# First feed-forward of a hybrid transformer block: its input products by seven half-size products, its output in pieces of two, two modulation vectors computed later

## Chip, cores, metric

One core of one Trainium2 chip runs the whole kernel. The metric is the device time of one execution in microseconds (us), the median of three runs. Engines are named as in the profile: PE (matrix multiplications; PEld is its loading of weights), DVE (vector), ACT (scalar), POOL, SP (which issues the DMAs).

## What is computed

One transformer block on 512 tokens `x` and 256 context tokens `ctx` of width 1024, all in float32. A vector `c` gives nine modulation vectors; each of the three stages normalises and modulates its input and adds its gated, normalised output:

```python
mod = (silu(c) @ w_ada + b_ada).reshape(B, 9, 1, 1024)          # mod_c likewise from c_ctx
swiglu = lambda h, w_in, w_out: (silu(h @ w_in[:, :2816]) * (h @ w_in[:, 2816:])) @ w_out
h  = rmsnorm(x, g0) * (1 + m[1]) + m[0];   x = x + 0.5 * m[2] * rmsnorm(swiglu(h, ffn1), p0)     # ctx too
h  = rmsnorm(x, g1) * (1 + m[4]) + m[3];   y = mixer(h, hc)     # window attention + gated scan, two merged
x  = x + m[5] * rmsnorm(y, p1)
h  = rmsnorm(x, g2) * (1 + m[7]) + m[6];   x = x + 0.5 * m[8] * rmsnorm(swiglu(h, ffn2), p2)
mixer's end:  y = (sigmoid(ga) * (o_att @ w_o_attn) + sigmoid(gr) * (o_rec @ w_o_hgrn)) @ w_out
```

## The kernel before

Every float32 operand of a product is split into a high part (a cast on ACT) and a low part (a subtraction on DVE), `split`, L64 to L66; a product is three matmuls, high by high, high by low, low by high (`mm3`, L71, L72, L74).

**FFN1** works on all 768 tokens. The 2816 columns between the layers are 22 tiles j of 128. For each j, `in_tile` in `ffn` makes the gate and the up projection: 8 steps over the width, each with 512 and 256 tokens of 3 matmuls, so 96 matmuls a tile. Its output `am` is split into `acth` and `actl`. The output product (`out_phase`) takes tiles in pieces, PIECES = (1, 3, 3, 3, 3, 3, 2, 4): for each of the six groups of 128 tokens and each tile of the piece 6 matmuls of 512 columns, summed in PSUM, and then added to `tok` on DVE (L369). A piece's output product is written behind the first input tile of the next piece. The last piece goes to `last1`, which finishes each token group and transposes it for the mixer (`post`, `pre_xn`, `make_hT`; this stretch is called the tail below).

**FFN2** works on 512 tokens, and makes its input products in another way, `ffn7`. After two ordinary tiles it computes each tile j by seven products of half the width by half the tokens (a Strassen-Winograd scheme): sums of quarters of the input (`sums2`, once) and of the weights (`weights`, L408 to L411, for each j), 7 x 4 x 3 = 84 matmuls of 256 tokens (`product`, L421 to L423), and additions of the results on DVE as they leave PSUM (L478 to L493). The quarters of the input, plain and summed, each split in two, are called forms.

**Modulation** is not done by PE. A generator goes through `w_ada` in tiles `wa` of 128 x 512 (two buffers) and multiplies and adds them into `macc` on DVE (L611, L613) for one or two vectors; a matmul with ones then sums over partitions, and the result is combined with `b_ada` (L658) or turned into columns (L636, L639). `tick(n)` runs such generators from the list `background` for n units of credit, one unit an accumulation. The first modulation is computed in the start. In FFN1's background stand gate 0 (x and ctx), columns 1 (x and ctx), gate 1 and columns 2; FFN2's background has gate 2.

**The mixer** ends in a merge loop: for each of 8 column tiles the two gates' projections and the two output projections, multiplied and added on DVE (L1100 to L1102) and split (`mgl`); then the y product with `w_out`.

Only the beginning is ordered by hand; from the first matmuls on a scheduler lays out each engine's instructions ahead of time, and each engine runs its own list in order. SP issues all DMAs of one list in order too, so a load that waits for its buffer holds up those behind it.

Of the kernel before, what the change touches and what calls it, by code (L numbers as in the profile page):

```python
# [43 lines left out]
def kernel(ctx: ExitStack, tc: tile.TileContext, i, out):  # L44
# [109 lines left out]
    xT = ct([P, KD, TA], "xT", pool=st)  # L154
# [80 lines left out]
    def make_hT(n, hh, hl, toks, xns, pool, tag="h32"):  # L235
# [9 lines left out]
        for k in range(KD):  # L245
# [57 lines left out]
    def ffn(w_in, w_out, hT, groups, ntok, pool, pieces, yacc, last, groups0=None, pre=None, ticks=0, final_pre=None,  # L303
            order=None):

        gmax = max(b - a for a, b in groups)
        early = []

        def in_w(j, u):
            return split_w(load_w(w_in[:, u * FF + j * P:u * FF + (j + 1) * P]))  # L310

        def in_tile(j):
            if j == 0:
                early.extend(proj_all(pre, hT, groups0 or groups, by_k=not groups0))
            gs_ = groups
            if early:
                g = early.pop(0)
            else:
                w = in_w(j, 0)
                tick(ticks)  # L320
                g = proj(w, hT, groups)
            if early:
                u = early.pop(0)
            else:
                w = in_w(j, 1)
                tick(ticks)
                u = proj(w, hT, groups)
            ah = ct([P, ntok * P], "acth", F32R, bufs=4, pool=pool)
            al = ct([P, ntok * P], "actl", F32R, bufs=4, pool=pool)
            for gp, up, (a, b) in zip(g, u, gs_):  # L330
                s = ct([P, gmax], "sg", bufs=2, pool=pool)
                nc.scalar.activation(s[:, :b - a], gp, AF.Silu)  # L332
                m = ct([P, gmax], "am", bufs=2, pool=pool)
                nc.vector.tensor_tensor(out=m[:, :b - a], in0=s[:, :b - a], in1=up, op=ALU.mult)  # L334
                split(ah[:, a:b], al[:, a:b], m[:, :b - a])
            return ah, al

        run_pieces(in_tile, w_out, ntok, pool, pieces, yacc, last, final_pre, order)

    def run_pieces(in_tile, w_out, ntok, pool, pieces, yacc, last, final_pre=None, order=None, w4=None):  # L340
# [52 lines left out]
    F_B11, F_B21, F_B22, F_U1, F_U2, F_T3, F_T4 = range(7)  # L393
    H4 = KD // 2

    def ffn7(w_in, w_out, forms, nt, ntok, pool, w4, pieces, yacc, last, pre, sums, nstd=2, ticks=0):
# [37 lines left out]
        def act(up):  # L434
            ah = ct([P, ntok * P], "acth", F32R, bufs=4, pool=pool)
            al = ct([P, ntok * P], "actl", F32R, bufs=4, pool=pool)
            split(ah, al, up.rearrange("p a b -> p (a b)"))
            return ah, al

        def std_tile(j):  # L440
            if j == 0:
                early.extend(ps() for _ in pre)
                for half in range(2):
                    for o, w in zip(early, pre):
                        std_half(o, w, half)
# [820 lines left out]
```

## Time and profile before

| | us |
|---|---|
| median of 3 runs (lowest to highest) | 1485.39 (1485.19 to 1489.04) |
| the profiled execution: own time | 1484.94 |
| the profiled execution: span in the trace | 1483.2 |
| mean granted PE clock, of full speed | 0.992 |
| FFN1, from the second input tile to the last input product | 67.80 to 579.98 |
| tail of FFN1 | 580 to 640 |
| merge loop and y product | 960 to 1166 |
| FFN2 | 1167 to the end |

The span lies 1.74 us inside the profiled execution's own time. An engine's busy time counts its instructions in execution; overlapping ones are counted once.

### The profile page before, as it was taken

What the parts mean: (1) busy time and instruction counts of PE and PEld (TensorE: products, weight loads), DVE (VectorE), ACT (ScalarE), POOL (GpSimd) and SP (SyncE); (2) the same over time, 40 slices, a digit from 0 to 9 for tenths busy, and PEclk for the clock granted to TensorE, in tenths of its full rate; (3) what the DMA queues carried; (4) which work ended last, traced back from release to release, by engine and by line L of the source; (5) the groups of instructions that cost most, each with busy time, mean ns of one, the idle gap of its engine ahead of it and who ended that gap; (6) DMA issues with size and microseconds to landing.
All of it is one profiled execution on the core that took longest, in us unless ns stands there. A gap on an engine that the chain in (4) does not pass through costs nothing.

```text
span 1483.2 us, 22466 instructions
## 1 busy us (share of the span) xinstructions
PE 1428.8 (96%) x9064; PEld 1227.1 (83%) x9064; DVE 982.1 (66%) x1601; ACT 583.2 (39%) x973; POOL 59.0 (4%) x87
## 2 busy tenths in 40 slices
PE   5999999999999999999999989999999999999997
PEld 2688888888888888788889867788778889999996
DVE  6856664675655333848578579853448987787785
ACT  6532121212121222543234468842237544454442
POOL 3200000000000000200000200000001000000001
PEclk9999999999999999999999989999999999999999
DMA  9564331454552211222122211023242643243211
GB/s 309 173 201 130 114 114 58 128 164 142 168 164 63 67 29 57 68 86 64 39 58 59 63 54 46 24 77 99 83 131 91 214 136 100 86 138 103 88 43 57
DMA packets 177904, 151.57 MB, mean 102 GB/s; under 512 B 6408, under 2 KB 152328, under 8 KB 177800
## 3 DMA queue, kind: packets, MB, share of 16 engines
q1 hardware_dynamic: 177800, 150.14, 33.3%
q8 instruction: 71, 1.16, 0.3%
q14 instruction: 33, 0.27, 0.1%
HBM read 148.02 MB, written 2.10 MB: 101 GB/s over the span
## 4 chain that ended last, share of the span: by engine, by line
PE 70%; issue 16%; DVE 7%; ACT 3%; DMA 2%; POOL 2%; DVEq 0%; POOLq 0%; ACTq 0%; SPq 0%
PE mm L71 18%; PE mm L74 18%; PE mm L72 18%; PE mm L421 2%; PE mm L423 2%; PE mm L422 2%; PE aux L421 2%; PE aux L422 2%; PE aux L423 2%; PE aux L1046 1%; POOL rs L227 1%; DVE wl L66 1%; DMA mx<-b_ada 1%; DMA wa<-w_ada 1%; POOL ss L226 1%
## 5 line engine op out<-in xcount | busy, mean ns | idle before, releaser
L71 PE MATMUL mm<-hh,wh 128*128 128x512 f32 (+1 forms) x1128 | 389.9, 347 | 0.5 <-ACT sg L332 0.2
L72 PE MATMUL mm<-hl,wh 128*128 128x512 f32 (+1 forms) x1128 | 368.9, 344 | 0.0
L74 PE MATMUL mm<-hh,wl 128*128 128x512 f32 (+1 forms) x1128 | 325.5, 346 | 0.7 <-DVE wl L66 0.7
L66 DVE TENSOR_TENSOR wl<-wraw,wh 128x1024 fp32r<-128x1024 f32 (+1 forms) x159 | 189.3, 1196 | 171.7 <-ACT wh L65 170.3
L65 ACT CAST wh<-wraw 128x1024 fp32r<-128x1024 f32 (+1 forms) x159 | 162.7, 1029 | 352.0 <-PE mm L72 238.0
L71 PEld LDWEIGHTS mm<-hh,wh 128*128 128x128 f32 x1128 | 212.6, 189 | 46.1 <-ACT gg L911 0.7
L72 PEld LDWEIGHTS mm<-hl,wh 128*128 128x128 f32 x1128 | 213.1, 189 | 27.4 <-DVE hl L541 0.6
L74 PEld LDWEIGHTS mm<-hh,wl 128*128 128x128 f32 x1128 | 185.8, 190 | 9.3 <-DVE wl L66 1.1
L71 PE MATMUL mm<-woh,acth 128*128 128x512 f32 x420 | 164.2, 391 | 0.9 <-DVE am L334 0.9
L72 PE MATMUL mm<-wol,acth 128*128 128x512 f32 x420 | 164.0, 391 | 0.0
L613 DVE SCALAR_TENSOR_TENSOR macc<-wa,cs,macc 128x512 f32<-128x512 f32 x140 | 101.7, 749 | 51.0 <-DMA wa<-w_ada 50.3
L74 PE MATMUL mm<-woh,actl 128*128 128x512 f32 x420 | 130.8, 390 | 0.0
L65 ACT CAST woh<-w 128x1024 fp32r<-128x1024 f32 x42 | 44.3, 1055 | 151.7 <-PE mm L74 149.0
L71 PEld LDWEIGHTS mm<-woh,acth 128*128 128x128 f32 x420 | 78.9, 188 | 18.1 <-DVE am L334 1.3
L74 PEld LDWEIGHTS mm<-woh,actl 128*128 128x128 f32 x420 | 78.8, 188 | 16.4
L72 PEld LDWEIGHTS mm<-wol,acth 128*128 128x128 f32 x420 | 78.9, 188 | 15.7
L369 DVE TENSOR_TENSOR tok<-tok,mm 128x512 f32<-128x512 f32 x96 | 61.5, 682 | 34.7 <-PE mm L74 34.7
L421 PE MATMUL mm<-hh,wh 128*128 128x256 f32 x240 | 68.3, 285 | 4.6 <-DVE sg L487 2.3
L421 PE MATMUL aux<-hh,wh 128*128 128x256 f32 x240 | 68.1, 284 | 0.4 <-ACT wh L65 0.4
L422 PE MATMUL aux<-hl,wh 128*128 128x256 f32 x240 | 67.9, 283 | 0.0
L423 PE MATMUL aux<-hh,wl 128*128 128x256 f32 x240 | 67.9, 283 | 0.0
L422 PE MATMUL mm<-hl,wh 128*128 128x256 f32 x240 | 67.8, 283 | 0.0
(342 smaller groups left out, 2472.0 us busy)
## 6 DMA issues: line engine op xcount, KB each, us to landing
wraw<-ffn_w_in SPq DMA_DIRECT2D x88, 512.0 KB, 4.1
wa<-w_ada SPq DMA_DIRECT2D x128, 256.0 KB, 3.0
w<-ffn_w_out SPq DMA_DIRECT2D x44, 512.0 KB, 4.3
wraw<-mix_w_in SPq DMA_DIRECT2D x42, 512.0 KB, 3.6
tok<-w_ada SPq DMA_DIRECT2D x16, 256.0 KB, 5.6
wraw<-w_out SPq DMA_DIRECT2D x8, 512.0 KB, 3.3
tok<-x SPq DMA_DIRECT2D x4, 512.0 KB, 8.0
wraw<-x SPq DMA_DIRECT2D x4, 512.0 KB, 3.4
```

Of the source, the lines that this page charges most:

```text
L65: nc.scalar.copy(hi, src)
L66: nc.vector.tensor_tensor(out=lo, in0=src, in1=f32(hi), op=ALU.subtract)
L71: nc.tensor.matmul(o, lhsT=sh, rhs=mh, start=start, stop=False)
L72: nc.tensor.matmul(o, lhsT=sh, rhs=ml, start=False, stop=False)
L74: nc.tensor.matmul(o, lhsT=sl, rhs=mh, start=False, stop=stop)
L226: nc.gpsimd.tensor_scalar(ss, ss, 1.0 / n, EPS, ALU.mult, ALU.add)
L227: nc.gpsimd.tensor_tensor(out=r, in0=ss, in1=mhalf, op=ALU.pow)
L369: nc.vector.tensor_tensor(out=y, in0=y, in1=o[h], op=ALU.add)
L421: nc.tensor.matmul(o, lhsT=wk, rhs=mh, start=first and k == 0, stop=False, skip_group_check=True)
L422: nc.tensor.matmul(o, lhsT=wk, rhs=ml, start=False, stop=False, skip_group_check=True)
L423: nc.tensor.matmul(o, lhsT=wl[:, k0 + k, :], rhs=mh, start=False, stop=k == H4 - 1, skip_group_check=True)
L613: nc.vector.scalar_tensor_tensor(out=a, in0=w, scalar=cs[:, v, k:k + 1], in1=a, op0=ALU.mult, op1=ALU.add)
```

## The change

FFN1 goes through `ffn7` too, on token halves of 384. `ffn` is gone. The forms become a class:

```diff
-    def ffn7(w_in, w_out, forms, nt, ntok, pool, w4, pieces, yacc, last, pre, sums, nstd=2, ticks=0):
+    class Forms:
+        def at(self, f, k, n=1):
+            if f <= F_T3:
+                return [e[f][:, k:k + n, :] for e in self.ext]
+            f -= F_B11
+            return [h[:, f % 2 * H4 + k:f % 2 * H4 + k + n, f // 2 * self.nt:(f // 2 + 1) * self.nt] for h in self.nat]
+        def sums(self, r11, r12, r21, r22, t4):
...
+            for b11, b12, b21, b22, z in zip(r11, r12, r21, r22, t4):
+                n = b11.shape[1]
+                nc.vector.tensor_tensor(out=b11, in0=b11, in1=b12, op=ALU.subtract)
+                nc.vector.tensor_tensor(out=b12, in0=b22, in1=b12, op=ALU.subtract)
+                nc.vector.scalar_tensor_tensor(out=b22, in0=b11, scalar=-1.0, in1=b22, op0=ALU.mult, op1=ALU.subtract)
+                split(*self.at(F_U2, k, n), b22)
+                split(*self.at(F_U1, k, n), b11)
+                split(*self.at(F_T3, k, n), b12)
+                nc.vector.scalar_tensor_tensor(out=z, in0=b22, scalar=-1.0, in1=b21, op0=ALU.mult, op1=ALU.subtract)
+                k += n
+    def ffn7(w_in, w_out, B, ntok, pool, w4, pieces, yacc, last, pre, sums, acts, by_k=False, nstd=2, ticks=0,
+             wo_bufs=3, final_pre=None, order=None):
...
         def product(o, w, k0, f, first=False):
             wh, wl = w
             for k in range(H4):
-                wk, mh, ml = wh[:, k0 + k, :], fh[:, f, k, :], fl[:, f, k, :]
+                wk = wh[:, k0 + k, :]
+                mh, ml = (m[:, 0, :] for m in B.at(f, k))
...
+            tick(ticks)
```

The call, the pieces, the raw output weights (they share the ring `wraw` of three buffers with the input weights) and the tiles of modulation, now 256 wide:

```diff
+    PIECES1 = (1, 2, 2, 2, 2, 2, 2, 2, 2, 2, 3)
-            raw = ct([P, D], "w4", bufs=4, pool=w4 or pool)
+            raw = ct([P, D], "w4", bufs=4, pool=w4) if w4 else ct([P, D], "wraw", bufs=3)
-            accs = [ct([P, 512], "macc", bufs=2, pool=pool) for _ in vs]
+        MW = 256
+            accs = [mod_tile("macc", pool) for _ in vs]
-                w = ct([P, 512], "wa", bufs=2, pool=pool)
+                w = mod_tile("wa", pool)
-        background += [mod_gate(0, (0, 1), 0.5, f1), mod_cols(1, (0, 1), f1),
-                       mod_gate(1, (0,), 1.0, f1), mod_cols(2, (0,), f1)]
+        background += [mod_gate(0, (0, 1), 0.5, f1), mod_cols(1, (0, 1), f1)]
-        ffn(i["ffn1_w_in"][0], i["ffn1_w_out"][0], (hh, hl), GROUPS, NT, f1, PIECES, tok, last1,
-            pre=pre1, ticks=4.2, final_pre=final_pre, order=ORDER)
+        ffn7(i["ffn1_w_in"][0], i["ffn1_w_out"][0], forms1, NT, f1, None, PIECES1, tok, last1, pre=pre1,
+             sums=(sums1, sums1_t4), acts=acts1, by_k=True, ticks=1.7, wo_bufs=2, final_pre=final_pre, order=ORDER)
```

Gate 1 and columns 2 move into the merge loop, with two accumulators and four tiles of `w_ada` in the buffers `b7h` and `b7l`:

```diff
+        mpool = {"macc": [b7[0][:, n] for n in (0, 1)], "wa": [b7[1][:, n] for n in range(4)], "mx": mg}
         for n in range(KD):
+            if n == 2:
+                background.extend([mod_gate(1, (0,), 1.0, mpool), mod_cols(2, (0,), mpool)])
...
                     gate(n, u, sigs[n])
+                    tick(6.5)
             if n:
                 merge(n - 1, sigs[n - 1][:, :T], sigs[n - 1][:, T:])
+                tick(6.5)
+        tick(1000)
         merge(KD - 1, sigs[KD - 1][:, :T], sigs[KD - 1][:, T:])
```

Left out of the diff: FFN2 uses the same class, with the sums in place, the multiplication of gate and up by halves, and ticks of 0.5 a product; the inputs' transposes `xT` are two tiles `act` whose buffers later hold FFN1's activations; the tail's scratch tiles lie in buffers that the forms leave.

Lines of the changed kernel: L382 to L387 the sums of the input, L412 to L414 those of the weights, L425 to L427 the products, L478 the ordinary tiles' multiplication, L503 to L509 the additions of product results, L640 and L642 modulation, L686 and L687 the gates.

**Start of FFN1, DVE.** First the list before, from the last split of the inputs on: the low part of second weights, the first tile's activation, the first output weights.

```order
L541 TENSOR_TENSOR hl_93<-h_126_494,hh_92 128x768
L66 TENSOR_TENSOR wl_706<-wraw_703,wh_705 128x1024
L334 TENSOR_TENSOR am_615<-sg_613,mm_513 128x512
L334 TENSOR_TENSOR am_621<-sg_619,mm_514 128x256
L66 TENSOR_TENSOR wol_628<-w_145_625,woh_627 128x1024
L66 TENSOR_TENSOR actl_612<-am_615,acth_611 128x512
L66 TENSOR_TENSOR actl_612<-am_621,acth_611 128x256
```

And the list of the change behind the first tile's multiplications: `fxl` are low parts of forms, `act` in L382 and L383 the inputs, `tok` in L387 the fourth sum.

```order
L66 TENSOR_TENSOR fxl_506<-act_93,fxh_505 128x768
L387 SCALAR_TENSOR_TENSOR tok_613<-act_93 128x768
L382 TENSOR_TENSOR act_92<-act_93,act_92 128x2x384
L66 TENSOR_TENSOR fxl_506<-act_92,fxh_505 128x768
L383 SCALAR_TENSOR_TENSOR act_93<-act_92,act_93 128x2x384
L66 TENSOR_TENSOR fxl_506<-act_92,fxh_505 128x768
L387 SCALAR_TENSOR_TENSOR tok_614<-act_93 128x768
L66 TENSOR_TENSOR fxl_506<-act_93,fxh_505 128x768
L66 TENSOR_TENSOR wol_642<-wraw_639,woh_641 128x1024
L66 TENSOR_TENSOR act_636<-up_607,act_635 128x768
L66 TENSOR_TENSOR wl_698<-wraw_695,wh_697 128x1024
```

The second weights of tile 1 (`wl_698`) stand behind the sums and splits of the whole input, the first output weights (`wol_642`) and tile 0's activation (`act_636`).

**FFN1 in the middle, DVE and SP.** First the list of DVE before, at the end of an output piece: additions to `tok`, low parts of weights, then gate by up of a tile.

```order
L369 TENSOR_TENSOR tok_508<-tok_508,mm_1447 128x512
L369 TENSOR_TENSOR tok_508<-tok_508,mm_1448 128x512
L66 TENSOR_TENSOR wol_1794<-w_347_1791,woh_1793 128x1024
L66 TENSOR_TENSOR wl_1682<-wraw_1679,wh_1681 128x1024
L334 TENSOR_TENSOR am_1605<-sg_1603,mm_1551 128x512
L334 TENSOR_TENSOR am_1611<-sg_1609,mm_1552 128x256
L66 TENSOR_TENSOR wl_1800<-wraw_1797,wh_1799 128x1024
L66 TENSOR_TENSOR actl_1602<-am_1605,acth_1601 128x512
L66 TENSOR_TENSOR actl_1602<-am_1611,acth_1601 128x256
L66 TENSOR_TENSOR wl_1864<-wraw_1861,wh_1863 128x1024
```

Then the list of DVE in the change, from the second chunk of gate 0 to the fifth result of a tile's products:

```order
L686 TENSOR_TENSOR gg_869<-aux_1400,mx_1470 128x256
L686 TENSOR_TENSOR gg_870<-aux_1407,mx_1470 128x256
L687 SCALAR_TENSOR_TENSOR gg_869<-gg_869,mx_1472 128x256
L687 SCALAR_TENSOR_TENSOR gg_870<-gg_870,mx_1472 128x256
L642 SCALAR_TENSOR_TENSOR macc_1478<-wa_1516,cs_78,macc_1478 128x256
L642 SCALAR_TENSOR_TENSOR macc_1479<-wa_1516,cs_78,macc_1479 128x256
L642 SCALAR_TENSOR_TENSOR macc_1478<-wa_1533,cs_78,macc_1478 128x256
L642 SCALAR_TENSOR_TENSOR macc_1479<-wa_1533,cs_78,macc_1479 128x256
L412 TENSOR_TENSOR wraw_1687<-wraw_1687 128x512
L413 TENSOR_TENSOR wraw_1685<-wraw_1685,wraw_1687 128x512
L503 TENSOR_TENSOR sg_1503<-sg_1503,mm_1453 128x384
L642 SCALAR_TENSOR_TENSOR macc_1478<-wa_1550,cs_78,macc_1478 128x256
```

And of the same place the list of SP in the change, with the loads that those instructions need (`mx` from `b_ada` and `norm_post`, `wa` from `w_ada`):

```order
L96 DMA wraw_1687<-ffn_w_in 128x8x128
L310 DMA wraw_1854<-ffn_w_out 128x1024
L681 DMA mx_1470<-b_ada 128x256
L683 DMA mx_1472<-norm_post 128x256
L637 DMA wa_1516<-w_ada 128x256
L637 DMA wa_1533<-w_ada 128x256
L637 DMA wa_1550<-w_ada 128x256
L637 DMA wa_1581<-w_ada 128x256
```

The addition of a product's result (L503), whose PSUM buffer PE fills again, now stands behind four accumulations that need `w_ada` loads and two gate additions that need the load of `b_ada`; on SP these loads stand behind one of output weights.

**End of the merge loop, DVE.** First the list before: one column tile.

```order
L1100 TENSOR_TENSOR gg_8440<-gg_8440,mm_9042 128x512
L1101 TENSOR_TENSOR gg_8440<-gg_8440,mm_9043 128x512
L1102 TENSOR_TENSOR gg_8440<-gg_8440 128x512
L66 TENSOR_TENSOR wl_9145<-wraw_9140,wh_9144 128x1024
L66 TENSOR_TENSOR mgl_9072<-gg_8440,mgh_9071 128x512
L66 TENSOR_TENSOR wl_9185<-wraw_9182,wh_9184 128x1024
L66 TENSOR_TENSOR wl_9217<-wraw_9214,wh_9216 128x1024
```

And the list of the change, in the last two column tiles but one:

```order
L1159 TENSOR_TENSOR w_1703_9779<-w_1703_9779,mm_10052 128x512
L664 TENSOR_TENSOR mx_9939<-aux_9932,ident_61 128x256
L642 SCALAR_TENSOR_TENSOR b7h_9119<-b7l_9120,cs_78,b7h_9119 128x256
L667 TENSOR_REDUCE mc_9500<-mx_9939 128x2
L642 SCALAR_TENSOR_TENSOR b7h_9119<-b7l_9120,cs_78,b7h_9119 128x256
L1160 TENSOR_TENSOR w_1703_9779<-w_1703_9779 128x512
L642 SCALAR_TENSOR_TENSOR b7h_9119<-b7l_9120,cs_78,b7h_9119 128x256
L1158 TENSOR_TENSOR w_1728_9944<-w_1728_9944,mm_10113 128x512
L642 SCALAR_TENSOR_TENSOR b7h_9119<-b7l_9120,cs_78,b7h_9119 128x256
L66 TENSOR_TENSOR mgl_10081<-w_1703_9779,mgh_10080 128x512
```

Between the multiplications of a column tile (L1158 to L1160) and its split (`mgl`) now stand accumulations of modulation.

## Rows read from the trace of the kernel before

**Rows 1.** The page: busy time of the engines, share of the span, instructions.

```profile
PE 1428.8 (96%) x9064; PEld 1227.1 (83%) x9064; DVE 982.1 (66%) x1601; ACT 583.2 (39%) x973; POOL 59.0 (4%) x87
...
PE 70%; issue 16%; DVE 7%; ACT 3%; DMA 2%; POOL 2%; DVEq 0%; POOLq 0%; ACTq 0%; SPq 0%
```

**Rows 2.** Windows by stage: us; busy us (instructions) of each engine; PEclk; DMA share; GB/s.

```profile
100.00:580.00 480.00, 480.00 (x2538) 410.59 (x2537) 265.60 (x392) 101.10 (x152) 0.00 (x0) 1.00 0.37 109
580.00:640.00 60.00, 54.78 (x311) 45.53 (x310) 46.57 (x90) 29.87 (x55) 12.06 (x24) 1.00 0.25 77
960.00:1060.00 100.00, 100.00 (x447) 81.35 (x448) 43.64 (x57) 34.58 (x48) 0.00 (x0) 1.00 0.31 90
1167.00:1225.00 58.00, 55.24 (x385) 51.00 (x385) 50.59 (x73) 26.07 (x42) 0.00 (x0) 1.00 0.50 150
1225.00:1425.00 200.00, 199.76 (x1365) 186.16 (x1365) 157.61 (x219) 90.99 (x139) 0.00 (x0) 1.00 0.34 101
```

**Rows 3.** Timeline of PE in FFN1 (start us, duration us): out product, last input products.

```profile
146.97 0.39 PE L71 MATMUL mm<-woh,acth 128*128 128x512 f32 x1
...
171.48 0.39 PE L71 MATMUL mm<-hh,wh 128*128 128x512 f32 x1
...
529.43 0.39 PE L71 MATMUL mm<-hh,wh 128*128 128x512 f32 x1
...
579.98 0.39 PE L71 MATMUL mm<-woh,acth 128*128 128x512 f32 x1
```

**Rows 4.** Timeline of PE in FFN2: out product, then two products of 256 columns.

```profile
1235.25 0.39 PE L71 MATMUL mm<-woh,acth 128*128 128x512 f32 x1
...
1251.61 0.28 PE L421 MATMUL mm<-hh,wh 128*128 128x256 f32 x1
...
1257.36 0.28 PE L421 MATMUL mm<-hh,wch 128*128 128x256 f32 x1
```

**Rows 5.** Timeline of DVE in FFN2: consecutive instructions.

```profile
1158.53 1.22 DVE L66 TENSOR_TENSOR wol<-w,woh 128x1024 fp32r<-128x1024 f32 x1
1159.67 0.42 DVE L487 TENSOR_TENSOR sg<-sg,mm 128x256 f32<-128x256 f32 x1
1160.00 0.68 DVE L408 TENSOR_TENSOR wc<-wraw,wraw 128x512 f32<-128x512 f32 x1
1160.60 0.41 DVE L489 TENSOR_TENSOR up<-up,aux 128x256 f32<-128x256 f32 x1
```

**Rows 6.** Groups of DVE in FFN1, 100 to 575: count, busy us, mean ns, idle before.

```profile
L613 DVE SCALAR_TENSOR_TENSOR macc<-wa,cs,macc 128x512 f32<-128x512 f32 x111 | 80.8, 749 | 47.5 <-DMA wa<-w_ada 46.9
...
L369 DVE TENSOR_TENSOR tok<-tok,mm 128x512 f32<-128x512 f32 x72 | 46.1, 682 | 30.7 <-PE mm L74 30.7
```

**Rows 7.** Start of FFN1: timeline of DVE, then PE, with idle time before.

```profile
62.88 0.96 DVE L541 TENSOR_TENSOR hl<-h,hh 128x768 fp32r<-128x768 f32 x1
...
67.80 0.50 PE L71 MATMUL mm<-hh,wh 128*128 128x512 f32 x1 [0.22 <-ACT sg L332]
...
87.19 0.51 PE L71 MATMUL mm<-woh,acth 128*128 128x512 f32 x1 [0.88 <-DVE am L334]
```

**Rows 8.** FFN2, timeline of PE: a stall.

```profile
1223.90 0.39 PE L421 MATMUL mm<-hh,wh 128*128 128x256 f32 x1 [1.52 <-DVE sg L487]
```

**Rows 9.** FFN1, waits: us in total, times, longest.

```profile
DVE macc L613 <- DMA wa<-w_ada: 50.3, 38, 3.5
...
DVE gg L658 <- DMA mx<-b_ada: 10.3, 4, 3.9
```

**Rows 10.** DMA issues in FFN1: count, KB each, median us to landing.

```profile
wa<-w_ada SPq DMA_DIRECT2D x86, 256.0 KB, 2.9
wraw<-ffn_w_in SPq DMA_DIRECT2D x34, 512.0 KB, 3.8
```

**Rows 11.** Tail of FFN1, timeline of DVE: first and last instruction.

```profile
585.46 0.69 DVE L672 TENSOR_TENSOR tok<-tok,mm 128x512 f32<-128x512 f32 x1 [2.24 <-PE mm L74]
...
637.46 0.42 DVE L258 TENSOR_TENSOR hl<-sg,hh 128x256 fp32r<-128x256 f32 x1
```

More of the change, by code (lines that the diff above doesn't have):

```diff
@@ L153 @@
     KQ = KD // NQ
-    xT = ct([P, KD, TA], "xT", pool=st)
+    xT = [ct([P, KH, TA], "act", bufs=2, pool=ax) for _ in range(2)]
     ab0 = ct([P, 2, KD, 2], "ab0", pool=st)
@@ L301, in tick, with run_pieces @@
                 background.pop(0)
[L303 to L340, printed above, removed]
+    def run_pieces(in_tile, w_out, ntok, pool, pieces, yacc, last, final_pre, order, w4, wo_bufs):
         order = order or range(ntok)
         def out_w(j):
-            raw = ct([P, D], "w4", bufs=4, pool=w4 or pool)
+            raw = ct([P, D], "w4", bufs=4, pool=w4) if w4 else ct([P, D], "wraw", bufs=3)
             nc.sync.dma_start(raw, w_out[j * P:(j + 1) * P, :])
@@ L441, in std_tile @@
             if j == 0:
[L442 to L445, printed above, removed]
+                early.extend(std_outs() for _ in (pre[:2] if by_k else pre))
+                if by_k:
+                    for k in range(KD):
+                        for o, w in zip(early, pre):
+                            std_k(o, w, k)
+                else:
+                    for h in range(2):
+                        for o, w in zip(early, pre):
+                            for k in range(KD):
+                                std_k(o, w, k, (h,))
+                ready = pre[len(early):]
+                del pre[:]
+                pre.extend(ready)
             gu = []
@@ L476, in in_tile @@
             nc.scalar.copy(up[:, 0, :], A)
-            product(B, g0, H4, F_B21, True)
-            nc.vector.tensor_tensor(out=up[:, 0, :], in0=up[:, 0, :], in1=B, op=ALU.add)
-            tick(ticks)
+            product(A2, g0, H4, F_B21, True)
+            nc.vector.tensor_tensor(out=up[:, 0, :], in0=up[:, 0, :], in1=A2, op=ALU.add)
             C = ps("aux")[:, :nt]
-            sg = ct([P, 2, nt], "sg", bufs=2, pool=pool)
+            sg = ct([P, 2, nt], "sg", pool=pool)
             product(A, g2, 0, F_U2)
@@ L493, in in_tile @@
             nc.vector.tensor_tensor(out=up, in0=sg, in1=up, op=ALU.mult)
[L494 to L496 removed]
+            return put_act(up)
+        run_pieces(in_tile, w_out, ntok, pool, pieces, yacc, last, final_pre, order, w4, wo_bufs)
     W = i["mix_w_in"][0]
@@ L659, in mod_gate, with sums1, sums1_t4, acts1 @@
                     nc.vector.scalar_tensor_tensor(out=g, in0=g, scalar=float(w), in1=gb, op0=ALU.mult, op1=ALU.mult)
-        hh2 = ct([P, KD, TA], "hh", F32R)
-        hl2 = ct([P, KD, TA], "hl", F32R)
+        N1 = TA // 2
+        ext = [ct([P, 3, H4, N1], tag, F32R, pool=f1) for tag in ("fxh", "fxl")]
+        forms1 = Forms(N1, (hh, hl), [[e[:, f] for f in range(3)] for e in ext])
+        act1 = []
+        def sums1():
+            t4 = [ct([P, 2, N1], "tok", bufs=6) for _ in range(2)]
+            blocks = [[x[:, k:k + 2, h * N1:(h + 1) * N1] for k in (0, 2)] for x in xT for h in range(2)]
+            forms1.sums(*blocks, t4)
+            act1.extend(ct([P, 4, TA], "act", F32R, bufs=2, pool=ax) for _ in range(2))
+        def sums1_t4():
+            forms1.last()
+            for t in ORDER:
+                tok[t] = ct([P, D], "tok", bufs=6)
+        slot = [0]
+        def acts1():
+            n = slot[0] % 4
+            slot[0] += 1
+            return [a[:, n, :] for a in act1]
+        h2 = []
         waiting = {}
         hts = []
+        scrs = []
         def post(t, o, n, v, w4, res):
             y = tok[t]
-            scr = ct([P, D], "w4", bufs=4, pool=w4)
+            if not scrs:
+                x4 = ct([P, 4, D], "fxh", pool=w4)
+                scrs.extend(x4[:, n, :] for n in range(4))
+            scr = scrs[t % 4]
             for h in range(2):
```

175 lines of the change are left out of this document (94 added, 81 removed).

## Prediction

> **What bounds the kernel now.** I read the page first for the busiest engine, then windows by stage, then PE's and DVE's timelines in the stages that the change touches, then the waits. PE is busy for 96% of the span and carries 70% of the chain that ended last [rows 1]. From 100 to 580 us, in FFN1, it is busy all the time, while DVE works 265.60 of 480 us, 55% [rows 2]. So fewer or shorter matmuls there are worth their full time, until DVE, whose instructions free PE's PSUM buffers and make the low parts of its weights, can no longer follow. Where that happens two stretches of FFN2 show, which already runs the seven products: with DVE at 157.61 of 200 us, 79%, PE loses 0.24 us; with DVE at 50.59 of 58 us, 87%, it loses 2.76 us, 4.8% [rows 2].
>
> **Products of FFN1.** The last three tiles' input products took 579.98 - 529.43 = 50.55 us, 16.85 us a tile, and an output product of three tiles 171.48 - 146.97 = 24.51 us, 8.17 us a tile [rows 3]. The new tile has 84 matmuls of 384 columns, a width that the trace does not show. In FFN2, 72 matmuls of 512 columns took 1251.61 - 1235.25 = 16.36 us, 0.2272 each, and 48 of 256 took 5.75 us, 0.1198 each [rows 4]. Halfway between lies 0.1735, in proportion to 512 columns 0.1704, to 256 columns 0.1797. I take the middle, since both neighbours are measured and the price has a fixed part: 84 x 0.1735 = 14.57 us (14.31 to 15.09). That saves 2.28 us in each of 20 tiles, **45.6 us** (35 to 51). The two ordinary tiles, 96 x 0.1735 = 16.66 us, give 0.4 more. Output products keep their count, 22 x 8.17 us, however cut into pieces.
>
> The Trainium skill's page "TensorE: Matmul & The Clock Gate", section "Back-to-back issue gap", gives columns / 2.4 + 2.5 ns for a matmul alone at full clock, 162.5 ns for 384 columns; by it the saving would be 64 us. The rows lie above it, 119.8 ns against its 109 and 227.2 against its 216, so I keep to them.
>
> **DVE beside them.** Prices: 0.42 us for 256 columns, 0.68 for 512, 1.22 for 1024 [rows 5], so about 0.55 for 384; an accumulation of 512 takes 0.749, an addition to `tok` 0.682 [rows 6]; with 256 fewer columns an accumulation is 0.749 - 0.26 = about 0.48; 768 columns take 0.96 [rows 7]. A tile now needs four splits of weights (3 x 1.22 + 0.68), four weight sums (2.7), three additions of results (1.65), one multiplication and split of 768 (1.9), one split of output weights (1.22) and six additions to `tok` (4.1): 20 instructions, 15.9 us. The additions cost half as much more a tile as in pieces of three. Modulation: the two vectors left are 24 chunk-versions of 9 credits, 216, paid with 7 x 1.7 = 11.9 a tile, so they fill 18 tiles; 192 accumulations (92 us), 24 splits (10) and 48 small instructions (21) make 6.8 us and 14.7 instructions a tile. Together 22.7 us in durations.
>
> Neighbours overlap: an instruction of 1.22 us was followed after 1.14, one of 0.68 after 0.60 [rows 5]. With 34.7 x 0.08 us less, DVE needs 19.9 us a tile. PE needs 14.57 + 8.17 + 0.3 (the matmuls with ones) = 23.06. That is 86%, just below the 87% of the bad stretch. Between the two stretches this is 4.2%, 0.97 us a tile, 17 us over 18 tiles. But 1.52 of the 2.76 us were one stall [rows 8]; without it the same line gives 1.9%, 8 us. I take the middle, **-12 us** (0 to -40).
>
> Where it will appear: the lists show the fifth product's addition (L503) behind gate additions and four accumulations. Behind that queue PE's seventh product waits for its PSUM buffer. The load of `b_ada` cost DVE 10.3 us in four waits in before [rows 9]; gate 0 has four such loads now, on SP behind a load of output weights. The shared ring is a second risk: the first weights of every other tile get their buffer only when G of the tile before is split, which the fourth product needs, at about 3 x 2.08 = 6.2 us; that leaves 14.57 - 6.2 - 3.8 (landing [rows 10]) = 4.5 us for the queue and the split. I cost it at nothing on that cover; late by more, it is paid in ten tiles.
>
> **Start.** DVE ends the inputs' splits at 63.84 us [rows 7]. In the new list eight instructions of 768 columns (some 7.3 us), the output weights (1.2) and the activation (0.9) stand between tile 0's multiplications, possible from about 67.8 us, and tile 1's second weights, which are so ready at about 79.5. PE, from 67.80 on [rows 7], has 8.3 us of first half and about 1 us of other matmuls, to 77. Before, it lost 0.88 here [rows 7]. That is **-3 us** net (0 to -5).
>
> **Tail.** The last piece holds three tiles instead of four: 8.17 us of PE work no longer covers DVE's finishing of tokens, which goes on from 585.46 to 637.46 [rows 11], with 46.57 us of work in those 60 [rows 2]. DVE's chain starts earlier in the shorter products and may shrink by some 5. **-3 us** (0 to -8).
>
> **Merge loop.** DVE works 43.64 of 100 us [rows 2]. Added are 96 accumulations (46 us), 12 splits, 4 gate pairs and 8 column pairs (15 us), less overlap of 124 x 0.08: 51 us over some 105. That is 92%, above the 87% stretch, so its 4.8% is the nearest price: **-5 us** (0 to -12). Whoever waits is PE, for the last `mgl`, which all y products need.
>
> FFN2 gets 16 more accumulations at 0.48 for 0.749, under 4 us of DVE behind PE at 79%: nothing (0 to -3).
>
> **Sum.** 45.6 + 0.4 - 12 - 3 - 3 - 5 = 23.0 us. 1483.2 - 23.0 = 1460.2 us of span, with the 1.74 us around it 1461.9, against 1484.94 of the profiled execution, which is 0.45 below the median of 1485.39. I predict **1462 us**.
>
> **Rivals.** *DVE covers it all.* PE loses only at the start and in the tail: 46 - 6 = 40 us, 1445, or 1440 with 0.1704. For it: PE lost almost nothing at 79%, and the products give DVE several us of slack within a tile. Against it: 86%.
>
> *DVE sets the pace.* Should its instructions in this mix not overlap, 22.7 us a tile, plus 0.6 for `b_ada` and 1.0 for part of the `wa` waits, make 24.3, 1.24 more than PE: -22 us, with the tail at -6 and the merge loop at -8: 46 - 22 - 3 - 6 - 8 = 7 us, 1478. For it: some pairs depend on each other. Against it: rows 5. The Trainium skill's page "VectorE: DVE Perf Modes", section "The DRAIN you can't avoid", speaks for this rival: the next instruction starts only when the pipe is empty, by which the durations add in full. The trace does not agree for independent neighbours (0.60 us between starts at 0.68 of duration), and the same page lets an instruction that is not held start earlier.
>
> *Loads hold DVE up, and the kernel is slower.* `wa` still has two buffers in FFN1, its loads share SP's list with weights that wait for a buffer, and 38 waits cost DVE 50.3 us in before, 1.3 each, over 111 accumulations [rows 6, 9]. They cost PE nothing, as DVE had 45% to spare. Now DVE has 23.06 - 19.9 = 3.2 us a tile, 57 us in 18 tiles, for 96 loads. At 1.3 us for each load it loses 125, 68 more than it can spare: 46 - 68 - 11 = -33, 1518. It decides from a mean wait of 57 + 35 = 92 us over 96 loads, 0.96 us. Against it: a 128 KB load should not land later than the 2.9 us of 256 KB [rows 10], and two accumulations a load come only every 4.3 us.
>
> **Chances.** Forecast 0.52 (1447 to 1476), DVE covers all 0.17, DVE sets the pace 0.18, loads 0.13. About 0.3%, 4.5 us, is what a measurement of this kernel can tell from no change. Of the third, a third ends within that; of the fourth, 0.03. So faster 0.81, same 0.09, slower 0.10. The range, 1440 to 1486, takes in the second and the third and leaves out the fourth and part of the second's good end.
>
> **What will show it.** Seven products' matmuls 0.1735 us apart and 14.6 us a tile where nothing waits; 8.2 us a tile of output; DVE busy 85% in FFN1 with PE idle about 0.7 us a tile, released by DVE (L503, L505) rather than by loads; a stall of 2 to 4 us around tile 1's second weights; PE no longer busy all the time in the merge loop. The prediction fails if 384 columns cost other than 0.170 to 0.180, if PE's idle time in FFN1 is near 0 or above 25 us, or if waits for `wa` exceed 1 us a load.

## The result, and the profile after

The changed kernel takes 1468.8 us, median of four runs (1466.95 to 1469.25), beside 1487.22 of the kernel before in the same comparison: a ratio of 0.9874, 95% interval 0.9854 to 0.9894, 18.4 us less. Its profiled execution spans 1466.5 us, 16.7 less than before. Cut at the same events of PE in both traces, those 16.7 us come from:

| stretch (PE's timeline) | before, us | after, us | difference | forecast |
|---|---|---|---|---|
| to the end of the first output product | 94.12 | 94.11 | 0.0 | +2.6 |
| to the beginning of FFN1's last output product | 485.86 | 449.10 | -36.8 | -25.4 |
| to the first copy of the mixer's `vt` on ACT (the tail) | 57.0 | 54.9 | -2.1 | -5.2 |
| to the last transposition of the attention | 331.8 | 332.3 | +0.5 | 0 |
| merge loop, to the first matmul of the y product | 99.44 | 111.24 | +11.8 | +5.0 |
| first part of the y product | 36.00 | 42.03 | +6.0 | in the line above |
| to the end | 378.95 | 382.83 | +3.9 | 0 |

The last piece has one tile less, so 8.17 us of output product stand in the second stretch after, in the third before. The forecast column has them so too.

The page of the changed kernel, its line of busy times (before: [rows 1]):

```profile
PE 1398.1 (95%) x8864; PEld 1233.1 (84%) x8864; DVE 1154.4 (79%) x2013; ACT 656.9 (45%) x1083; POOL 60.9 (4%) x87
```

Its windows, columns as in [rows 2]: first by stage, FFN1, tail, merge loop, first part of the y product, beginning and rest of FFN2; then four of 3 us from the y product's beginning:

```profile
100.00:540.00 440.00, 439.02 (x2323) 409.37 (x2323) 374.18 (x634) 159.21 (x235) 0.00 (x0) 1.00 0.33 99
540.00:600.00 60.00, 52.25 (x278) 42.35 (x277) 48.03 (x89) 30.86 (x55) 15.81 (x24) 0.95 0.27 85
930.40:1041.64 111.24, 103.52 (x449) 80.92 (x447) 86.17 (x168) 34.70 (x49) 0.00 (x0) 1.00 0.65 191
1041.64:1083.67 42.03, 37.33 (x150) 28.85 (x148) 23.90 (x36) 14.45 (x22) 1.47 (x4) 0.92 0.53 159
1110.00:1136.00 26.00, 22.70 (x149) 20.98 (x149) 24.52 (x38) 21.40 (x37) 0.00 (x0) 0.93 0.56 181
1136.00:1400.00 264.00, 259.24 (x1814) 242.74 (x1813) 212.75 (x316) 122.43 (x192) 0.00 (x0) 1.00 0.39 116
...
1043.00:1046.00 3.00, 0.57 (x2) 0.19 (x1) 3.00 (x9) 1.68 (x3) 0.00 (x0) 0.86 0.47 139
1046.00:1049.00 3.00, 1.40 (x3) 1.16 (x4) 3.00 (x6) 0.00 (x0) 0.00 (x0) 0.50 0.37 96
1049.00:1052.00 3.00, 3.00 (x8) 2.31 (x7) 2.01 (x4) 1.07 (x2) 0.00 (x0) 0.50 0.85 274
1052.00:1055.00 3.00, 3.00 (x15) 2.32 (x14) 2.22 (x4) 0.28 (x1) 0.00 (x0) 1.00 0.90 261
```

FFN1 is the reader's first surprise: DVE is busy 374.18 of 440 us, 85%, as forecast (86%), and PE is idle for 0.98 us. In the merge loop it is the other way round: DVE has 77%, less than in FFN1, and PE loses 7.7. Its timeline, with the idle time before an instruction and what ended it (before: [rows 3, 4, 7, 8]):

```profile
79.03 0.50 PE L71 MATMUL mm<-woh,act 128*128 128x512 f32 x1 [0.44 <-ACT tok L332]
...
540.09 0.33 PE L425 MATMUL aux<-hh,wh 128*128 128x384 f32 x1
...
542.69 0.33 PE L425 MATMUL mm<-hh,wh 128*128 128x384 f32 x1
...
543.21 0.39 PE L71 MATMUL mm<-woh,act 128*128 128x512 f32 x1
...
957.95 0.38 PE L651 MATMUL aux<-mx,ones 128*128 128x256 f32 x1 [0.59 <-ACT mx L65]
...
960.59 0.39 PE L652 MATMUL aux<-mx,ones 128*128 128x256 f32 x1 [1.80 <-DVE mx L66]
...
990.62 0.39 PE L651 MATMUL aux<-mx,ones 128*128 128x256 f32 x1 [1.15 <-ACT mx L65]
...
1047.60 1.22 PE L72 MATMUL mm<-wol,mgh 128*128 128x512 f32 x2 [3.80 <-DVE wol L66]
...
1121.57 0.38 PE L425 MATMUL aux<-hh,wh 128*128 128x256 f32 x1 [2.03 <-ACT wh L65]
...
1123.30 0.39 PE L74 MATMUL mm<-hh,wl 128*128 128x256 f32 x1 [1.22 <-DVE wl L66]
...
1156.18 0.39 PE L425 MATMUL mm<-hh,wh 128*128 128x256 f32 x1 [1.73 <-DVE sg L503]
```

From 540.09 to 542.69 lie fifteen matmuls of 384 columns, 0.1733 us each, against 0.1735 forecast. Just before it needs the low part of tile 1's second weights, at 79.03, PE waited 0.44 us, and not for them: the wait is for ACT's copy of an output product's result (L332). In the merge loop every stall stands before a matmul with ones (L651, L652): seven of them, 7.5 us. At 1047.60 PE waits 3.80 us for the low part of the first output weights `wol`. The last three rows are FFN2's beginning: 2.03 us for the high part of the weights of a product that stands ahead in PE's list, 1.22 for the low part of tile 1's second weights, and 1.73 for an addition of a product's result (L503).

DVE's timeline of the same kernel, at the start, at both ends of the tail (before: [rows 7, 11]), at the first output weights and in FFN2:

```profile
77.72 2.35 DVE L66 TENSOR_TENSOR wl<-wraw,wh 128x1024 fp32r<-128x1024 f32 x2
...
548.87 1.29 DVE L727 TENSOR_TENSOR tok<-tok,mm 128x512 f32<-128x512 f32 x2 [0.59 <-PE mm L74]
...
598.60 0.42 DVE L260 TENSOR_TENSOR hl<-wcl,hh 128x256 fp32r<-128x256 f32 x1
...
1046.33 1.22 DVE L66 TENSOR_TENSOR wol<-wraw,woh 128x1024 fp32r<-128x1024 f32 x1
...
1154.44 0.48 DVE L642 SCALAR_TENSOR_TENSOR macc<-wa,cs,macc 128x256 f32<-128x256 f32 x1 [1.71 <-DMA wa<-w_ada]
```

While PE waits at the beginning of the y product, DVE is busy without a gap (3.00 of 3.00 us from 1043 to 1046 and from 1046 to 1049): `wol` stands in its list behind accumulations of modulation, with which it is late. In FFN2 DVE waits 1.71 us for a load of `w_ada` (1154.44) just ahead of the addition for which PE waits 1.73 us.

The waits, in FFN1 up to 560 us (two lines; before: [rows 9]) and in the merge loop (four): us in total, times, longest.

```profile
DVE sg L503 <- PE mm L427: 10.5, 7, 4.0
...
DVE macc L642 <- DMA wa<-w_ada: 9.9, 14, 3.0
...
DVE b7h L642 <- DMA b7l<-w_ada: 7.7, 9, 2.2
...
PE aux L651 <- ACT mx L65: 4.6, 5, 1.5
...
DVE b7h L640 <- DMA b7l<-w_ada: 4.4, 3, 2.4
...
PE aux L652 <- DVE mx L66: 3.0, 2, 1.8
```

DVE waits for results of PE in FFN1 (L503), which is how it looks when PE sets the pace. Loads of `wa` cost it 9.9 us there, but 12.1 in a quarter of that time in the merge loop, where they go to `b7l`.

### The profile page after: what moved, and what is told of

It is laid out like the page before. It is cut to its first block, busy times and chain, and to the rows that moved or that the text cites. A ratio compares the mean times of both kernels' runs of the same rounds, so it can differ in the third digit from the quotient of the medians.

```text
span 1466.5 us, 22992 instructions
## 1 busy us (share of the span) xinstructions
PE 1398.1 (95%) x8864; PEld 1233.1 (84%) x8864; DVE 1154.4 (79%) x2013; ACT 656.9 (45%) x1083; POOL 60.9 (4%) x87
## 5 line engine op out<-in xcount | busy, mean ns | idle before, releaser
L71 PE MATMUL mm<-hh,wh 128*128 128x512 f32 (+2 forms) x488 | 172.1, 356 | 0.3 <-ACT gg L967 0.2
L72 PE MATMUL mm<-hl,wh 128*128 128x512 f32 (+2 forms) x488 | 168.3, 353 | 0.1
L74 PE MATMUL mm<-hh,wl 128*128 128x512 f32 (+2 forms) x488 | 160.4, 359 | 3.4 <-DVE wl L66 3.4
L425 PE MATMUL mm<-hh,wh 128*128 128x256 f32 (+1 forms) x400 | 122.8, 307 | 5.3 <-DVE sg L503 5.1
L425 PE MATMUL aux<-hh,wh 128*128 128x256 f32 (+1 forms) x400 | 121.8, 304 | 2.0 <-ACT wh L65 2.0
L427 PE MATMUL aux<-hh,wl 128*128 128x256 f32 (+1 forms) x400 | 121.6, 304 | 0.0
L427 PE MATMUL mm<-hh,wl 128*128 128x256 f32 (+1 forms) x400 | 121.5, 304 | 0.0
L426 PE MATMUL aux<-hl,wh 128*128 128x256 f32 (+1 forms) x400 | 121.5, 304 | 0.0
L426 PE MATMUL mm<-hl,wh 128*128 128x256 f32 (+1 forms) x400 | 121.4, 304 | 0.0
L642 DVE SCALAR_TENSOR_TENSOR macc<-wa,cs,macc 128x256 f32<-128x256 f32 x196 | 88.0, 479 | 17.6 <-DMA wa<-w_ada 16.6
L71 PE MATMUL mm<-woh,act 128*128 128x512 f32 x252 | 98.9, 393 | 0.5 <-ACT tok L332 0.4
L74 PEld LDWEIGHTS mm<-hh,wl 128*128 128x128 f32 x488 | 89.1, 192 | 11.1 <-DVE wl L66 3.9
L425 PEld LDWEIGHTS mm<-hh,wh 128*128 128x128 f32 x400 | 75.9, 190 | 9.1 <-DVE sg L503 7.9
L74 PE MATMUL mm<-woh,act 128*128 128x512 f32 x252 | 78.1, 390 | 0.1
L425 PEld LDWEIGHTS aux<-hh,wh 128*128 128x128 f32 x400 | 75.9, 190 | 2.5 <-ACT wh L65 2.5
```

Of the source, the lines that this page charges most:

```text
L71: nc.tensor.matmul(o, lhsT=sh, rhs=mh, start=start, stop=False)
L72: nc.tensor.matmul(o, lhsT=sh, rhs=ml, start=False, stop=False)
L74: nc.tensor.matmul(o, lhsT=sl, rhs=mh, start=False, stop=stop)
L425: nc.tensor.matmul(o, lhsT=wk, rhs=mh, start=first and k == 0, stop=False, skip_group_check=True)
L426: nc.tensor.matmul(o, lhsT=wk, rhs=ml, start=False, stop=False, skip_group_check=True)
L427: nc.tensor.matmul(o, lhsT=wl[:, k0 + k, :], rhs=mh, start=False, stop=k == H4 - 1, skip_group_check=True)
```

## The experiments

All edits are to the changed kernel; its 1468.8 us is the number to compare with. The kernel before ran beside experiments 1 to 4, 5 to 8 and 9 to 11 at 1486.88, 1487.38 and 1488.19 us, so a difference of 1 us between these groups says nothing.

**1. The two vectors in the merge loop left out.**

```diff
-                background.extend([mod_gate(1, (0,), 1.0, mpool), mod_cols(2, (0,), mpool)])
+                gg[1, 0], mcol[2, 0] = gg[0, 0], mcol[1, 0]
```

> The changed kernel, in which the two vectors moved into the merge loop are not computed at all (gate 0 and columns 1 stand in for them, so 96 accumulations with their loads and 24 matmuls with ones are left out). Theory (the modulation in the merge loop costs about 12 us there and 6 us at the beginning of the y product): 1468.8 - 18 = 1451 us, 1448 to 1455, merge loop back to about 100 us with PE never idle. Rival (the loss in these stages has another cause, such as buffers or the order of weights): 1462 or more.

Measured: 1453.27 us (1451.47 to 1454.75), ratio to before 0.9779 (0.976 to 0.9799). The merge loop in its windows:

```profile
932.01:1031.44 99.43, 99.43 (x435) 80.90 (x434) 39.73 (x47) 32.69 (x42) 0.00 (x0) 1.00 0.29 85
```

PE is busy in all of the 99.43 us, and the first part of the y product is back at 35.91. So the 17.8 us that these two stretches had lost are the price of the modulation there, as the theory has it; in the loop, 7.5 are PE's stalls, and PE's busy time is 4.1 lower without the matmuls with ones (99.43 for 103.52). The whole gain is smaller, 15.5 us: in its profiled execution the mixer begins 2.0 us later, and the part behind the y product is 1.6 us longer.

**2. The matmuls with ones later in the program** (`mid` is what follows the accumulations of the chunk before: its matmuls with ones and the instructions on their result).

```diff
                 yield len(vs)
+                if mid and k == 3:
+                    mid()
```

> The changed kernel, but for vectors of one version the matmuls with ones stand half a chunk later in the program, behind four accumulations of the next chunk. Theory (PE stands in its own list before matmuls with ones whose operands DVE and ACT have not finished, 7.8 us in the merge loop): these waits fall below 2 us, the loop takes 100 to 104 us instead of 111, the kernel 1457 to 1463 us. Rival (DVE is simply too busy in the loop): the waits turn up before the splits of weights or of the merged tiles, loop 108 us or more, kernel 1466 to 1470.

Measured: 1467.36 us (1465.34 to 1470.71), loop 111.94, stalls 5.4 us in PE's timeline, among them:

```profile
961.94 0.39 PE L659 MATMUL aux<-mx,ones 128*128 128x256 f32 x1 [0.65 <-ACT mx L65]
...
964.77 0.56 PE L660 MATMUL aux<-mx,ones 128*128 128x256 f32 x1 [1.99 <-DVE mx L66]
```

The edit didn't do what it says: the scheduler set the matmuls with ones in PE's list within ten places of where they had been. The run says nothing about the theory; what it shows is that the place of an instruction in the program is not its place in the list.

**3. All four vectors in FFN1** (with ticks of 2.4).

```diff
-                background.extend([mod_gate(1, (0,), 1.0, mpool), mod_cols(2, (0,), mpool)])
...
-        background += [mod_gate(0, (0, 1), 0.5, f1), mod_cols(1, (0, 1), f1)]
+        background += [mod_gate(0, (0, 1), 0.5, f1), mod_cols(1, (0, 1), f1),
+                       mod_gate(1, (0,), 1.0, f1), mod_cols(2, (0,), f1)]
```

> The changed kernel with gate 1 and columns 2 back in FFN1 (2.4 credits a product instead of 1.7), still in tiles of 256. DVE was busy some 87% in the middle of FFN1 and gets 51 to 61 us more over 440, to 98 to 100%. Theory (DVE at 87% costs PE nothing in FFN1, at 98% and more it sets the pace): 18 us back in merge loop and y product, 5 to 20 us lost in FFN1, 1456 to 1471 us. Rival (PE loses in FFN1 from 87% on, as read from FFN2's beginning): over 25 us lost, above 1476. Second rival (DVE hides all of it): 1449 to 1455.

Measured: 1478.63 us (1478.28 to 1481.52), 0.9947 (0.9929 to 0.9965). Its windows of FFN1 and tail, then its waits in FFN1:

```profile
100.00:540.00 440.00, 428.86 (x2245) 393.24 (x2244) 403.96 (x734) 154.96 (x233) 0.00 (x0) 1.00 0.41 121
540.00:600.00 60.00, 52.05 (x240) 44.42 (x239) 39.92 (x66) 20.66 (x34) 4.84 (x10) 0.91 0.31 99
```

```profile
DVE macc L642 <- DMA wa<-w_ada: 13.5, 20, 1.5
...
PE aux L651 <- ACT mx L65: 3.6, 6, 1.3
...
PE mm L425 <- DVE sg L503: 3.4, 4, 1.7
...
PE mm L71 <- DVE tok L334: 2.6, 2, 2.3
```

The merge loop is back at 99.42 us. DVE is busy 92% in FFN1 and stands another 3% before loads, and PE loses 11.1 us in 440, at sums with ones, at product results and at output products. The sums take the largest part, 4.9 us (L651 and L652), as in the merge loop. From 540 us on the last vector holds up the last products (one wait before a sum is 4.32 us), and the tail's first addition to a token comes at 581.4 us, 550.2 in experiment 1. By its total, 25 us above experiment 1, the rival came out and the theory did not; but the loss does not begin at 87%, as the next run shows. The theory's bound, 98%, was set too high: at 92% PE already loses time, in part to DVE's additions, in part to sums that are late.

**4. Gate 1 alone in FFN1** (`mod_gate(1, (0,), 1.0, f1)` in FFN1's background, ticks of 1.9; the merge loop keeps columns 2).

> The changed kernel with gate 1 alone back in FFN1 (1.9 credits a product), columns 2 still in the merge loop: DVE in FFN1 gets 17 to 20 us more, to about 91%. Theory (the loss in the merge loop goes with its matmuls with ones, 24 to 16, and FFN1 has room at 91%): 18 us of loss become about 11, FFN1 the same, 1460 to 1464 us. Rival (FFN1 loses steeply above 87%): 6 us or more lost in FFN1, 1466 us or more.

Measured: 1464.59 us (1462.18 to 1467.66), 0.9857 (0.9833 to 0.9882); loop 108.19, first part of the y product 35.89, its FFN1:

```profile
100.00:540.00 440.00, 437.11 (x2316) 407.59 (x2315) 389.25 (x679) 160.20 (x238) 0.00 (x0) 1.00 0.37 110
```

The total lies between theory and rival. At 88% PE loses 2.9 us, where the rival asked for 6 or more and the theory for nothing. With 85, 88 and 92% (runs after, 4 and 3) the loss is 1.0, 2.9 and 11.1 us in 440. These are not prices of DVE's busy share alone: more vectors also bring more loads and more sums, and 1.3 of the 2.9 us stand before matmuls with ones. No run separates the two.

**5. One load of `w_ada` for a chunk in the merge loop.**

```diff
-                w = mod_tile("wa", pool)
+                if k == 0 or not isinstance(pool, dict):
+                    w = mod_tile("wa", pool)
```

> The changed kernel, but in the merge loop only the first of a chunk's eight tiles of w_ada is loaded and serves all eight accumulations (the other 84 loads are left out; DVE's work and the 24 matmuls with ones stay). Theory (PE waits before the matmuls with ones because DVE waits for these loads, 12 us in the loop): loop 100 to 103 us instead of 111, kernel 1454 to 1459 us. Rival (DVE's own work or its order makes them late): loop 108 to 111, kernel 1465 to 1470.

Measured: 1458.38 us (1457.91 to 1459.64), 0.9808 (0.9794 to 0.9823). The merge loop:

```profile
932.76:1038.00 105.24, 102.48 (x452) 81.89 (x451) 88.35 (x184) 36.11 (x52) 0.00 (x0) 1.00 0.37 105
```

DVE has the same work, 88 us in a shorter loop, and PE's stalls fall from 7.7 to 2.8 us; the first part of the y product is back at 35.88. So the loads made the sums late, and not DVE's work, for 5 of the 7.7 us; the other 2.8, which keep the loop above the theory's 100 to 103, stay open. Of the 17.9 us between experiment 1 and the changed kernel in these two stretches, 12.2 go with the loads.

**6. The matmuls with ones left out in the merge loop.**

```diff
+                if isinstance(pool, dict):
+                    outs.append(f32(lo))
+                    continue
                 nc.tensor.matmul(o, lhsT=ones, rhs=hi, start=True, stop=False)
```

> The changed kernel, but in the merge loop the 24 matmuls with ones are left out (the low part of the sum goes on in their place; DVE's work and all loads stay). Theory (PE loses its time in the loop only by standing before these matmuls): loop 100 to 102 us, the late low part of the first output weights stays, kernel 1457 to 1461 us. Rival (without them PE waits for splits of weights or of merged tiles, which DVE makes late): loop 106 us or more, kernel 1464 to 1470.

Measured: 1462.63 us (1459.86 to 1466.7), 0.9838 (0.9815 to 0.986); loop 109.39 us. By its loop the rival came out; its total lies between the two ranges. PE's longest wait, and ACT's list ahead of what it waits for:

```profile
PE aux L71 <- ACT woh L65: 7.4, 1, 7.4
```

```profile
1032.95 0.41 ACT L65 CAST mx<-b7h 128x256 fp32r<-128x256 f32 x1 [7.68 <-DVE b7h L642]
...
1037.16 0.62 ACT L65 CAST mgh<-w 128x512 fp32r<-128x512 f32 x1 [3.80 <-DVE w L1163]
```

PE's stalls within the loop are gone but for 2.3 us; one of 7.4 us appears at its end, where the first output weights stand on ACT behind splits (`mx`, `mgh`) that wait for DVE, 7.68 us for accumulations and 3.80 for a merged tile. Without the sums PE meets the late modulation one step later, through another queue. How much of that is late loads (DVE waits 2.19 us for one just ahead, at 1030.82) and how much DVE's own work, this run does not show.

**7. Six buffers for `w_ada` in the merge loop.**

```diff
-"wa": [b7[1][:, n] for n in range(4)]
+"wa": [b7[1][:, n] for n in range(4)] + [b7[0][:, n] for n in (2, 3)]
```

> The changed kernel with six buffers for tiles of w_ada in the merge loop instead of four (two lie in the unused half of b7h). Theory (the loads make DVE late): DVE's waits for them fall from 12 us to 6 or less, PE's in the loop from 7.8 to 4 or less, kernel 1463 to 1466 us. Rival (the loads are late because of their place in SP's list or of the queue itself): no change, 1467 to 1470.

Measured: 1461.1 us (1459.43 to 1462.77), 0.9822 (0.9805 to 0.9838); loop 107.58, first part of the y product 35.88. Waits in the loop:

```profile
DVE b7h L642 <- DMA b7l<-w_ada: 2.7, 5, 0.9
...
PE aux L651 <- ACT mx L65: 2.4, 4, 1.1
...
PE aux L652 <- DVE mx L66: 1.7, 1, 1.7
...
DVE b7h L640 <- DMA b7l<-w_ada: 1.6, 1, 1.6
```

DVE's waits for these loads go from 12.1 to 4.3 us, PE's stalls from 7.5 to 4.1, with every load and every sum still there; the time is 2 us below the theory's range. The memory of the two buffers had lain unused.

**8. FFN1's last piece of four** (`PIECES1 = (1, 2, 2, 2, 2, 2, 2, 2, 2, 1, 4)`, the last two output weights in the ring `wh`).

> The changed kernel with FFN1's pieces (1, 2, 2, 2, 2, 2, 2, 2, 2, 1, 4): the last output product has 8.17 us more PE work beside DVE's finishing of the tokens. Theory (the tail is bounded by DVE's chain over six token groups, the piece of three took cover away): 4 to 6 us back, less half a microsecond for one more piece, kernel 1463 to 1466 us. Rival (the tail is bounded by something that the piece does not move): 1468 to 1470.

Measured: 1466.73 us (1462.96 to 1468.56), 0.986 (0.9841 to 0.9879), between theory and rival, and not clearly faster than 1468.8. DVE's chain in the tail:

```profile
542.43 1.29 DVE L727 TENSOR_TENSOR tok<-tok,mm 128x512 f32<-128x512 f32 x2 [0.59 <-PE mm L74]
...
597.91 0.42 DVE L260 TENSOR_TENSOR hl<-wcl,hh 128x256 fp32r<-128x256 f32 x1
```

It takes 55.9 us here, 50.2 in the changed kernel, 52.4 before. With the longer product its last addition to a token (L727) comes 41.0 us after the first instead of 32.5, and the mixer begins only 0.7 us earlier. So no more than some 2 us of what the piece of three lost come back.

**9 to 11. Put together.** Nine is experiment 4 with experiment 7; eleven adds experiment 8 to ten; ten is nine and

```diff
-                if j == 0:
+                if j == (0 if by_k else nstd - 1):
                     sums[0]()
```

> The changed kernel with gate 1 back in FFN1 and six buffers for columns 2 in the merge loop. Theory (the loop's loss goes with late loads of w_ada, so that fewer loads and more buffers both reduce it; FFN1 takes gate 1 for about 3 us): loop 102 to 105 us, y product at its old 35.9, kernel 1457 to 1461 us. Rival (the two edits remove the same waits and FFN1's loss stays): 1461 to 1465.

> The same, and in FFN2 the sums of the input stand behind tile 1's weights in the program, so that the low part of its second weights comes ahead of most of them on DVE. Theory (3.25 us of PE's wait at FFN2's beginning come from that low part, which the change put behind the sums): this wait falls to 1 us or less, 2 to 3 us faster than the run before it. Rival (the first products then wait for the forms instead): no difference.

> The same as the run before, and FFN1's last piece of four. Theory (the tail is DVE's chain over the token groups, 50 us, which grows when DVE waits for later products, so the piece gives back little): 0 to 2 us faster. Rival (cover for the chain is worth its PE time): 4 us or more faster.

Measured, for nine, ten and eleven: 1460.45 us (1456.94 to 1467.22; 0.9804, 0.9788 to 0.982) with a loop of 105.81; 1458.01 (1456.44 to 1458.1; 0.9796, 0.9783 to 0.981); 1458.41 (1456.17 to 1460.53; 0.9801, 0.9786 to 0.9816). The two edits of nine remove partly the same waits: together they are not clearly better than experiment 7 alone, at the boundary of theory and rival. Ten's beginning of FFN2:

```profile
1116.78 0.39 PE L427 MATMUL aux<-hh,wl 128*128 128x256 f32 x1 [0.18 <-DVE wl L66]
...
1122.31 0.50 PE L71 MATMUL mm<-woh,acth 128*128 128x512 f32 x1 [1.02 <-ACT tok L332]
...
1127.61 0.38 PE L425 MATMUL aux<-hh,wh 128*128 128x256 f32 x1 [0.86 <-ACT wh L65]
```

The wait for the low part of the second weights has become 0.18 us, as the theory had it, but waits of 1.02 us for the copy of an output product's result and of 0.86 for the products' weights have come: 2.06 us in place of 3.25. The medians differ by 2.4 us, in the span of what the runs scatter. Eleven is no faster than ten; the theory had 0 to 2 us. Ten is faster than both kernels, 1458.1 at most against 1466.95 at least.

## Why the forecast held, and where its steps failed

The time, 1468.8, lies in the likeliest case's own range, 1447 to 1476, and the gain is 18 us for 23 forecast. Two terms of the sum were wrong in opposite directions and hid one another: by the table, the stretch up to the last output product saved 11.4 us more than forecast, the merge loop and the y product lost 12.8 more. That the time came out so near is luck.

*The matmuls of 384 columns* were right: 0.1733 us each, and the second stretch saved 36.8 + 8.17 = 44.9 us for the 45.6 that the sum had there before losses. The Trainium skill's page "TensorE: Matmul & The Clock Gate", section "Back-to-back issue gap", gives columns / 2.4 + 2.5 ns, so 0.1625 us, for one alone; the trace stays above it.

*DVE beside them*: its load was right (86% forecast, 85% measured), the price of it wrong. I took the 4.8% that PE lost in FFN2's beginning at 87% for the effect of a busy DVE. In FFN1 85% cost 1.0 us and not 12. The prediction had named idle time near 0 as a sign that it fails, and by that sign this step failed. What the stretch in FFN2 had lost stands in DVE's timeline of the kernel before, just ahead of the stall of 1.52 us [rows 8]:

```profile
1221.62 0.69 DVE L658 TENSOR_TENSOR gg<-aux,mx 128x512 f32<-128x512 f32 x1 [1.47 <-DMA mx<-b_ada]
...
1223.43 0.41 DVE L487 TENSOR_TENSOR sg<-sg,mm 128x256 f32<-128x256 f32 x1
```

DVE stood 1.47 us for the load of `b_ada`, and the addition that PE waited for came behind it. A second stall of the stretch, 0.53 us at 1186.55, came behind 1.21 us that DVE waited for a load of weights. These two are 2.05 of the 2.76 us, and the changed kernel shows the like in FFN2 (1154.44, 1156.18). So what I had read as the price of a busy DVE was in the main that of loads in its list. In FFN1 no single wait of DVE for a load of modulation was above 1.3 us from 100 to 540 us; that PE lost so little there for this reason is not shown. The rival in which DVE covers it all was right for this stage. By the Trainium skill's page "VectorE: DVE Perf Modes", section "The DRAIN you can't avoid", durations would have added to 98%, an estimate from 22.7 of 23.06 us (PE's terms add up to 23.04, which changes nothing). The trace doesn't agree: from 100 to 540 us the durations of DVE's 634 instructions add up to some 415 us, 94%, and it is busy for 374.18, 85%.

*Start*: tile 1's second weights were ready at 78.9 us, 79.5 forecast. PE came to them at 79.37 and did not wait for them, where I had some 3 us, since the first output products and a product of the next tile stood ahead of them in its list. I had counted 1 us of such work; it was 2.7, and 0.44 us of waiting for ACT. In FFN2's beginning, where I had forecast nothing of the kind, late weights cost 3.25 us (1121.57, 1123.30) for 0.41 at the same place before; ten moves the low part forward and keeps 2.06 us of waits.

*Tail*: -6.1 us for -3. DVE's chain shrank by some 2 us, from 52.4 to 50.2, where I gave it 5; with the 8.17 us of cover gone this makes the 6.1.

*Merge loop*: -17.8 us for -5, outside my bound of 12. The step that failed is its mechanism. I priced DVE's load, 92%, and DVE was busy 77%. What cost PE its time in the loop are sums whose accumulations wait for loads: PE meets them in its list and holds up everything behind. At the y product PE stood behind DVE, as I had it, but for the output weights and not for the last `mgl`; by then DVE was working off what had come late, and where the loads came earlier (experiments 5 and 7) this stall was gone too. That is the third rival's mechanism, set in the wrong stage: in FFN1 88 loads came in 440 us, one every 5.0, and served two vectors each; in the loop 91 in 111, one every 1.2, for one vector each, with four buffers. Experiments 5 and 7 show the loads as the cause of most of it; experiment 2 could not, and experiment 6 leaves a part to DVE's own work. How the 12.1 us divide between the number of buffers and the place of the loads in SP's list stays open: six buffers left 4.3.

*DVE sets the pace* (second rival) did not happen here; experiment 3 comes nearest to it. It is also the products' change alone, with the vectors where they had been but in tiles of 256: 8 us faster than before. The move of two vectors brought 10 more, net of the 18 that it cost where they went.

## What to carry to other kernels

Background work that ends in an instruction of the busiest engine puts that engine behind all of the background's waits: count buffers of its loads before its instructions. A share of busy time from one stretch prices another only if the stalls in it come from that share; look at what each of them waited for. When work moves, price the stage that takes it by that stage's own queues: here the stage that it left kept its saving, and the stage that took it lost 18 us.

## What the hardware showed beside

Within PE's stall of 3.80 us at the y product's beginning (1043.80 to 1047.60) the granted clock fell: it was 0.86 in the window from 1043 to 1046 us, 0.50 (1.2 GHz) from 1046 to 1052 and 1.00 (2.4 GHz) from 1052, so that 4.4 busy us were spent at half speed, some 2.2 us (an estimate) on top of the 3.80. In the loop, stalls of up to 1.80 us left it at 1.00. In experiment 2 one of 1.99 just behind one of 0.65 was followed by a mean of 0.72 from 964 to 970 us, and in FFN2's beginning the two stalls of 2.03 and 1.22 by 0.66 from 1125 to 1128; in ten, with three shorter ones, it stayed at 1.00 from 1113 to 1134.

Loads of 128 KB landed 2.1 us after issue in FFN1, where the DMA engines were busy 0.33, and 2.7 in the merge loop, at 0.65; those of 256 KB had taken 2.9 in FFN1 [rows 10].
